# One plain round of the first feed-forward matrix instead of two, and six accumulators of the output projection held between its last two passes

## The chip, the cores and the metric

The kernel runs on one core of a Trainium2 chip. The metric is the device time of one execution in microseconds. A core has a matrix engine (PE, TensorE), three engines for element-wise work (DVE or VectorE, ACT or ScalarE, POOL or GpSimd) and a queue engine that issues most loads (SP). Matrix products are accumulated in PSUM, which has eight banks of 128 partitions x 512 float32; everything else lies in SBUF.

## What is computed

Two layers of an encoder trunk on x of 512 frames x 1024 features, all in float32. Each layer mixes three groups of heads (windowed attention, forgetting attention, mLSTM) and then applies a feed-forward part:

```python
def _layer(x, norm1, w_in, ..., w_out, norm2, w_ff1, w_ff2):
    z = _rms(x, norm1) @ w_in
    ...
    x = x + jnp.concatenate([ya, yb, yc], axis=-1) @ w_out
    u = _rms(x, norm2) @ w_ff1
    return x + jnp.square(jax.nn.relu(u)) @ w_ff2
```

ya has the features 0 to 511 of the concatenation, yb 512 to 767, yc 768 to 1023. In tiles of 128 that is k = 0 to 3, 4 and 5, 6 and 7. w_out is 1024 x 1024, w_ff1 1024 x 4096, w_ff2 4096 x 1024.

## The kernel before

**Products in three parts.** Every large operand is split into a rounded half `hi` and a rest `lo`, and a product is three matmuls, hi x hi, hi x lo and lo x hi (`mm3`, L262 to L265). Weights come by DMA as tiles of 128 x 1024 (a *job*). `prep_part` makes `whi` on ScalarE (L205) and `wlo` on VectorE (L206). `getjob` hands out the next job in the order of the list `jobs` and has the two after it prepared; three pairs of `whi` and `wlo` exist. `load_ahead` keeps the loads going as far as there are free buffers (three `raw`, and in the feed-forward four `fraw` and, later, `xt` and `ms`).

**Output projection.** The last part of the generator `big_work` (L573 to L592) runs over the passes of `WPASS`, k = 0 to 3, then 4 and 5, then 6 and 7, and in each over four column groups `hf` of 256 features. Each group takes two banks. At the end of each group in each pass, VectorE adds the two banks to the residual `xT` (L587). In the last pass `xprep` then makes the halves `xh` (ScalarE, L334) and `xl` (VectorE, L335) of the gained x, which the feed-forward reads. The marks `wo0`, `wo1` and `wo2` tell when a pass has been issued. After `wo0`, `c_tail(0)` transposes the first half of the mLSTM output (L1007) and splits it as k = 6 (L1008, L1009); after `wo1`, `c_tail(1)` does so with the second half, k = 7. Then the buffers of the mixing part are released, those of the feed-forward opened, and the third pass is issued.

**Feed-forward, first matrix.** The 4096 hidden features are cut into `NR` = 8 rounds of 512, two to a group `s`. A round runs in one of two ways. The plain way (`ff1_std`, L1214) multiplies everything: four units of one job and 48 matmuls of 256 columns. The other way (`ff1_st`, L1245) is Strassen's, in Winograd's form: seven units of one job and 24 matmuls of 256 columns, on sums of blocks of x and of the weights. The sums of x come from `xsums` (L350) in eight steps. Those of the weights come partly from a second load that adds in the buffer (L160, issued by GpSimd) and partly from VectorE (L216 and L220). Both ways leave the squared ReLU in `ct`, from which `csplit`, `n1_`, `n2_`, `gsplit` and `tail_` (L1180 to L1206) make sums and their halves for the second matrix. The first `NSTD` = 2 rounds are plain.

In the Strassen way the sixth unit's bank X is read by VectorE (L1270), and the seventh unit adds to the same bank.

**Feed-forward, second matrix.** `ff2(s)` (L1306) runs Strassen's way over group s, 14 units of 24 matmuls, seven for each half `dg` of the output. VectorE adds each result to `xT` (L1294). Group 0 first multiplies the residual by `nv`, minus the mean square of x (L1293); the last group multiplies by `r2`, its reciprocal (L1296). So the second norm is applied after the matrices.

**The order.** L1359 to L1377 set it: first the 4 x `NSTD` plain units, with `sqacc` after the first of them (the sum of the squares, L326 to L330), `xsums` from the second on, two steps a unit, and `emit_r2` (L1121) after the fourth, which makes `nv` and `r2`. Then `ff_pairs` (L117) takes turns between units of `ff2` and of the remaining rounds; `LEAD` rounds' units could go ahead, and `LEAD` is 0. The order on each engine is set when the program is built: by and large the order of the code, with work moved ahead where an engine would wait.

Of the kernel before, what the change touches and what calls it, by code (L numbers as in the profile page):

```python
# [16 lines left out]
ALU = mybir.AluOpType  # L17
# [28 lines left out]
NSTD = 2  # L46
# [4 lines left out]
def trunk(ctx, tc, x, cols, rows, gate_w, tabs, w_in, w_out, w1, w2, out):  # L51
# [49 lines left out]
    LEAD = 0  # L101
# [349 lines left out]
    for l in range(L):  # L451
# [79 lines left out]
        def big_work():  # L531
# [41 lines left out]
            for pi, (a, b) in enumerate(WPASS):  # L573
                for hf in range(4):
                    ps = [att() for _ in range(2)]
                    if b - a == 4 or hf % 2 == 0:
                        ws = getjob()
                    for k in range(a, b):
                        hi, lo = ws[k - a if b - a == 4 else hf % 2 * 2 + k - a]
                        for j in range(2):  # L580
                            cs_ = slice(j * P, (j + 1) * P)
                            mm3(ps[j], hi[:, cs_], lo[:, cs_], yhi(k), ylo(k), k == a, k == b - 1)
                        if k < b - 1:
                            yield 1.31
                    for j in range(2):
                        kx = hf * 2 + j
                        V.tensor_tensor(xT[:, kx], ps[j], xT[:, kx], ALU.add)  # L587
                        if pi == len(WPASS) - 1:
                            xprep(kx, g2(l, kx), xh, xl)
                    if hf == 3:  # L590
                        done.add(f"wo{pi}")
                    yield 1.31  # L592

# [500 lines left out]
        fill_to("wo1")  # L1094
        c_tail(1)
        close_phase()
# [19 lines left out]
        def bank():  # L1116
            return banks.popleft()
# [3 lines left out]
        def emit_r2():  # L1121
# [7 lines left out]
            A.activation(r2, lnv, AF.Exp, scale=-1.0)  # L1129
            V.tensor_tensor(lnv, nv, r2, ALU.mult)  # L1130
            V.scalar_tensor_tensor(r2, lnv, 2.0, r2, ALU.add, ALU.mult)
            rr_.update(nv=nv, r2=r2)
# [81 lines left out]
        def ff1_std(s, rr):  # L1214
            for i in range(2):
# [3 lines left out]
                for j in range(2):  # L1219
# [10 lines left out]
                    if j == 1:  # L1230
# [7 lines left out]
                        else:  # L1238
                            if rr:
                                units.extend(quads)  # L1240
# [4 lines left out]
        def ff1_st(s, rr):  # L1245
            X, Y = bank(), bank()
# [59 lines left out]
        def ff2(s):  # L1306
# [37 lines left out]
            for dg in range(2):  # L1344
# [10 lines left out]
                if s == 0 and dg:  # L1355
                    free_ff.append(ms_)
# [5 lines left out]
        for n_ in range(4 * NSTD):  # L1362
            next(gens[1])
            if n_ == 0:
                for kx in range(KT):
                    sqacc(kx, kx == 0)
            if n_ == 3:
                emit_r2()
            if n_ == 1:
# [6 lines left out]
        for which, u in ff_pairs():  # L1376
            next(gens[which])  # L1377
# [61 lines left out]
```

## Time and profile before

| | |
|---|---|
| runs shown | 1065.3, 1065.5, 1065.88 us, median 1065.5 |
| profiled execution, its own time | 1065.74 us |
| its span, first to last instruction | 1064.0 us |
| granted TensorE clock | 1.00 |
| loads in the feed-forward | 512 KB each, median 4.2 to 5.1 us to landing by SP, 6.3 to 7.8 by GpSimd |
| HBM, read and written | 147.86 MB and 2.13 MB |

The page of the profile gives times in microseconds, unless marked ns. L1294 is line 1294 of the kernel. "out<-in" names tiles without their numbers; all PSUM tiles are called `at`. A row of a timeline has the start, the duration, the engine, the line and the operation, and in brackets how long the engine had been idle before it and what ended that. Matmuls are pipelined and their ends modelled, so the distance from start to start tells more than the duration. VectorE's rows overlap by about 0.1 us in the same way.

### The profile page before, as it was taken

To read this page: it belongs to the slowest core of one execution; us is meant where nothing else is said; L and a number is where in the kernel's file an instruction comes from. 1 tells how busy PE (TensorE), PEld (TensorE's weight loads), DVE (VectorE), ACT (ScalarE), POOL (GpSimd) and SP (SyncE) were. 2 spreads that over 40 slices of the span, in tenths; PEclk is the share of its full clock that TensorE was granted. 3 is DMA by queue.
4 is the path that set the end of the run, shared out by engine and by line. 5 is a ranking of instruction groups with operands and counts; after the bars stand their busy time and mean duration, and the time that the engine had idled before them with its cause. 6 is when DMAs were issued, how large, how long until landed. Compare 5 with 4: busy or idle time off the path is not lost.

```text
span 1064.0 us, 21687 instructions
## 1 busy us (share of the span) xinstructions
PE 1053.7 (99%) x8768; PEld 1002.8 (94%) x8768; DVE 904.2 (85%) x1540; ACT 627.4 (59%) x1097; POOL 102.3 (10%) x154
## 2 busy tenths in 40 slices
PE   8999999999999999999999999999999999999998
PEld 8999977899999999999999998778999999999998
DVE  7696877899997988988977878688999888898797
ACT  6446655376666666567455467444766666666662
POOL 2030020100010000010002200101000101001000
PEclk9999999999999999999999999999999999999999
DMA  6523121165388687676135221213544886767752
GB/s 215 166 98 110 61 68 51 61 193 144 120 211 224 161 217 199 179 215 181 51 110 164 94 80 41 85 46 134 145 120 140 221 215 173 222 181 190 212 134 80
DMA packets 47365, 151.86 MB, mean 143 GB/s; under 512 B 5648, under 2 KB 8848, under 8 KB 47264
## 3 DMA queue, kind: packets, MB, share of 16 engines
q1 hardware_dynamic: 39056, 120.84, 34.0%
q0 software_dynamic: 8064, 29.36, 15.9%
q8 instruction: 69, 1.13, 0.4%
q14 instruction: 32, 0.26, 0.1%
q10 hardware_dynamic: 144, 0.26, 0.1%
HBM read 147.86 MB, written 2.13 MB: 141 GB/s over the span
## 4 chain that ended last, share of the span: by engine, by line
PE 85%; DVE 9%; ACT 3%; issue 1%; DMA 0%; SPq 0%; DVEq 0%
PE at L263 26%; PE at L265 26%; PE at L264 26%; DVE rt L726 2%; DVE wlo L206 2%; PE at L856 1%; PE at L898 1%; PE at L881 1%; ACT pe L769 1%; PE at L979 1%; DVE z L722 1%; DVE z L728 1%; PE at L756 1%; DMA raw<-in_w_in_dram 0%; DVE rb L407 0%
## 5 line engine op out<-in xcount | busy, mean ns | idle before, releaser
L205 ACT ACTIVATE whi<-raw 128x1024 fp32r<-128x1024 f32 (+1 forms) x130 | 136.2, 1048 | 114.6 <-PE at L264 87.8
L264 PE MATMUL at<-xhl,whi 128*128 128x256 f32 (+1 forms) x704 | 198.0, 281 | 0.0
L263 PE MATMUL at<-xhl,whi 128*128 128x256 f32 (+1 forms) x640 | 181.4, 283 | 0.0
L265 PE MATMUL at<-xhl,wlo 128*128 128x256 f32 (+1 forms) x640 | 180.4, 282 | 0.0
L263 PE MATMUL at<-yg,whi 128*128 128x256 f32 (+1 forms) x592 | 179.9, 307 | 0.5 <-DVE xT L1294 0.5
L206 DVE TENSOR_TENSOR wlo<-raw,whi 128x1024 fp32r<-128x1024 f32 (+1 forms) x130 | 157.4, 1211 | 27.0 <-ACT whi L205 26.6
L265 PE MATMUL at<-yg,wlo 128*128 128x256 f32 (+1 forms) x592 | 178.4, 301 | 0.0
L264 PE MATMUL at<-yg,whi 128*128 128x256 f32 (+1 forms) x560 | 169.4, 303 | 0.0
L263 PE MATMUL at<-whi,xhl 128*128 128x256 f32 (+1 forms) x576 | 163.0, 283 | 0.8 <-ACT xhl L334 0.7
L265 PE MATMUL at<-whi,xhl 128*128 128x256 f32 (+1 forms) x576 | 160.5, 279 | 0.6 <-DVE xhl L335 0.6
L264 PE MATMUL at<-wlo,xhl 128*128 128x256 f32 (+1 forms) x576 | 160.3, 278 | 0.5 <-DVE wlo L206 0.5
L205 ACT ACTIVATE whi<-fraw 128x1024 fp32r<-128x1024 f32 x100 | 106.1, 1061 | 83.9 <-PE at L264 79.6
L206 DVE TENSOR_TENSOR wlo<-fraw,whi 128x1024 fp32r<-128x1024 f32 x100 | 122.2, 1222 | 26.2 <-ACT whi L205 25.6
L264 PEld LDWEIGHTS at<-xhl,whi 128*128 128x128 f32 x704 | 132.2, 188 | 1.8 <-issue 0.5
L263 PEld LDWEIGHTS at<-xhl,whi 128*128 128x128 f32 x640 | 120.1, 188 | 1.7 <-ACT ct L1232 0.5
L265 PEld LDWEIGHTS at<-xhl,wlo 128*128 128x128 f32 x640 | 120.1, 188 | 1.2
L263 PEld LDWEIGHTS at<-yg,whi 128*128 128x128 f32 x592 | 111.2, 188 | 6.3 <-issue 1.7
L265 PEld LDWEIGHTS at<-yg,wlo 128*128 128x128 f32 x592 | 111.1, 188 | 5.3
L263 PEld LDWEIGHTS at<-whi,xhl 128*128 128x128 f32 x576 | 108.2, 188 | 1.8 <-ACT xhl L334 0.9
L264 PEld LDWEIGHTS at<-yg,whi 128*128 128x128 f32 x560 | 105.2, 188 | 4.2 <-DVE yg L1009 0.5
L265 PEld LDWEIGHTS at<-whi,xhl 128*128 128x128 f32 x576 | 108.2, 188 | 1.1 <-DVE xhl L335 1.0
L264 PEld LDWEIGHTS at<-wlo,xhl 128*128 128x128 f32 x576 | 108.4, 188 | 0.7 <-DVE wlo L206 0.7
(301 smaller groups left out, 2517.0 us busy)
## 6 DMA issues: line engine op xcount, KB each, us to landing
fraw<-in_w_dram SPq DMA_DIRECT2D x72, 512.0 KB, 4.9
raw<-in_w_dram SPq DMA_DIRECT2D x56, 512.0 KB, 4.3
raw<-in_w_in_dram SPq DMA_DIRECT2D x34, 512.0 KB, 3.5
fraw<-in_w_dram POOLq DMA_DIRECT2D x32, 512.0 KB, 6.3
raw<-in_w_out_dram SPq DMA_DIRECT2D x16, 512.0 KB, 3.2
xt<-in_w_dram SPq DMA_DIRECT2D x16, 512.0 KB, 5.1
raw<-in_w_dram POOLq DMA_DIRECT2D x14, 512.0 KB, 7.2
ms<-in_w_dram SPq DMA_DIRECT2D x12, 512.0 KB, 4.2
```

The lines of the kernel that those rows point to most:

```text
L205: A.activation(hi[:, cs_], raw[:, cs_], AF.Copy)
L206: V.tensor_tensor(lo[:, cs_], raw[:, cs_], hi[:, cs_], ALU.subtract)
L263: T.matmul(o, sh, mh, start=first, stop=False, skip_group_check=skip)
L264: T.matmul(o, sh, ml, start=False, stop=False, skip_group_check=skip)
L265: T.matmul(o, sl, mh, start=False, stop=last, skip_group_check=skip)
L722: V.tensor_tensor(z10, z10, bc(rq), ALU.mult)
L726: V.tensor_tensor(r10[:, oo:oo + n, a:a + 32], z10[:, oo:oo + n, b:b + 32], tb(S_, n, a, a + 32), ALU.mult)
L728: V.tensor_tensor(zaq[t], ro[:, :640], rt[:, :640], ALU.add)
L756: T.matmul(sc[r][:, g * 256:g * 256 + nk], qTA[g][r * 64:(r + 1) * 64, c * P:(c + 1) * P], kTA[r * 64:(r + 1) * 64, k0:k0 + nk], start=Tru ...
L769: A.activation(pe[:, u, :nk], sc[u % 2][:, (u // 2) * 256:(u // 2) * 256 + nk], AF.Exp, bias=nmx[:, u:u + 1], accum_out=ssum[:, u:u + 1])
L856: T.matmul(sp[:, :nk], qTB[rs, pr, n * P:(n + 1) * P], kTB[rs, pr, :nk], start=True, stop=False)
L881: T.transpose(pt[:, b * P:(b + 1) * P], scs[r][:, b * P:(b + 1) * P], ident)
```

## The change

`NSTD` becomes 1: the second round of each layer is computed in Strassen's way instead of the plain one. `LEAD` becomes 7: the seven units of that round run ahead of the first unit of `ff2`. `xsums` begins after the first plain unit and is through after the fourth; `sqacc` moves to behind the first Strassen unit and `emit_r2` to behind the fourth. The last two instructions of `emit_r2`, a correction of `r2`, become `finish_r2` and move to the end of `ff2(0)`. A bank that ScalarE seeds must be one that a matmul has written before.

In the output projection the first pass stays. Then the column groups 0, 1 and 2 take k = 4 and 5 into six banks that stay open, with `c_tail(1)` issued after the second of them, and `c_tail(0)` ahead of them as before. After the release of the buffers, groups 2, 0 and 1 take k = 6 and 7 into the same banks, and group 3 takes k = 4 to 7 at once. The host lays out the jobs of `w_out` to match, in the same number and size.

```diff
-NSTD = 2
+NSTD = 1
...
-    LEAD = 0
+    LEAD = 7
...
+            open_ = {}
+            for hf in range(3):
+                open_[hf] = [att() for _ in range(2)]
+                if hf != 1:
+                    ws = getjob()
+                for k in (4, 5):
+                    wo_part(open_[hf], ws[2 * (hf % 2) + k - 4], k, k == 4, False)
+                    if k == 5:
+                        done.add(f"wo1{hf}")
                     yield 1.31
+            for hf in (2, 0, 1, 3):
+                if hf == 3:
+                    open_[hf] = [att() for _ in range(2)]
+                if hf in (0, 3):
+                    ws = getjob()
+                for k in range(4 if hf == 3 else 6, 8):
+                    wo_part(open_[hf], ws[k - 4 if hf == 3 else (hf if hf < 2 else 1) * 2 + k - 6], k, hf == 3 and k == 4,
+                            k == 7)
+                    if k < 7:
+                        yield 1.31
+                wo_out(open_[hf], hf, True)
+                if hf == 3:
+                    done.add("wo2")
+                yield 1.31
...
-        fill_to("wo1")
+        fill_to("wo11")
         c_tail(1)
+        fill_to("wo12")
...
-        def bank():
-            return banks.popleft()
+        full = set()
+
+        def bank(seeded=False):
+            b = next(b for b in banks if not seeded or id(b) in full)
+            banks.remove(b)
+            full.add(id(b))
+            return b
...
+            rr_.update(nv=nv, lnv=lnv, r2=r2)
+
+        def finish_r2():
+            nv, lnv, r2 = (rr_[n] for n in ("nv", "lnv", "r2"))
             V.tensor_tensor(lnv, nv, r2, ALU.mult)
             V.scalar_tensor_tensor(r2, lnv, 2.0, r2, ALU.add, ALU.mult)
-            rr_.update(nv=nv, r2=r2)
...
-            X, Y = bank(), bank()
+            X, Y = bank(), bank(True)
...
                 if s == 0 and dg:
+                    finish_r2()
                     free_ff.append(ms_)
...
-        for n_ in range(4 * NSTD):
-            next(gens[1])
+        for n_, (which, u) in enumerate([(1, None)] * 4 * NSTD + list(ff_pairs())):
+            next(gens[which])
             if n_ == 0:
+                xt_ = wt("xt", "xt")
+                bg = xsums(l, *(v3(xt_[:, i * S:(i + 1) * S], 256) for i in range(2)))
+            if n_ < 4:
+                next(bg)
+                next(bg)
+            if n_ == 4:
                 for kx in range(KT):
                     sqacc(kx, kx == 0)
-            if n_ == 3:
+                free_ff.append(xt_)
+            if n_ == 7:
                 emit_r2()
```

`wo_part` holds the two `mm3` of a column group for one k, and `wo_out` the two adds of L587 and, where asked, `xprep`; both were written in place before.

More of the change, by code (lines that the diff above doesn't have):

```diff
@@ L572, in big_work, with wo_part @@
                 yield 1.31
[L573 to L591, printed above, removed]
-                    yield 1.31
+            def wo_part(ps, tiles, k, first, stop):
+                hi, lo = tiles
+                for j in range(2):
+                    cs_ = slice(j * P, (j + 1) * P)
+                    mm3(ps[j], hi[:, cs_], lo[:, cs_], yhi(k), ylo(k), first, stop)
@@ new lines, in wo_out @@
+            def wo_out(ps, hf, full):
+                for j in range(2):
+                    kx = hf * 2 + j
+                    V.tensor_tensor(xT[:, kx], ps[j], xT[:, kx], ALU.add)
+                    if full:
+                        xprep(kx, g2(l, kx), xh, xl)
+            for hf in range(4):
+                ps = [att() for _ in range(2)]
+                ws = getjob()
+                for k in range(4):
+                    wo_part(ps, ws[k], k, k == 0, k == 3)
+                    if k < 3:
+                        yield 1.31
+                wo_out(ps, hf, False)
+                if hf == 3:
+                    done.add("wo0")
+                yield 1.31
@@ L1238, in ff1_std @@
                         else:
-                            if rr:
+                            if rr == NSTD - 1:
                                 units.extend(quads)
@@ L1361, in trunk @@
         bg = None
-        for n_ in range(4 * NSTD):
-            next(gens[1])
+        for n_, (which, u) in enumerate([(1, None)] * 4 * NSTD + list(ff_pairs())):
+            next(gens[which])
             if n_ == 0:
+                xt_ = wt("xt", "xt")
[4 more added lines that the diff above has]
+            if n_ == 4:
                 for kx in range(KT):
                     sqacc(kx, kx == 0)
-            if n_ == 3:
+                free_ff.append(xt_)
+            if n_ == 7:
                 emit_r2()
-            if n_ == 1:
-                xt_ = wt("xt", "xt")
-                bg = xsums(l, *(v3(xt_[:, i * S:(i + 1) * S], 256) for i in range(2)))
-            if bg is not None:
-                next(bg, None)
-                next(bg, None)
-        free_ff.append(xt_)
-        for which, u in ff_pairs():
-            next(gens[which])
         close_phase()
@@ L1413, in _layout @@
         c = w_out[l].reshape(D, 4, 256).transpose(1, 0, 2)
-        t = [tiles(c, a, b - a) for a, b in WPASS]
-        wo.append(cc([t[0]] + [cc([t_[0::2], t_[1::2]], 2) for t_ in t[1:]], 0))
+        t, u, v = (tiles(c, a, b - a) for a, b in WPASS)
+        two = [cc(p, 1) for p in ((u[0], u[1]), (u[2], v[2]), (v[0], v[1]), (u[3], v[3]))]
+        wo.append(cc([t, np.stack(two)], 0))
     wo = np.stack(wo)
```

4 lines of the change are left out of this document (added).

## The prediction

> **What bounds the kernel now.** I read the page first: its busy shares, its forty slices, and the chain that ended last.
>
> ```profile
> PE 1053.7 (99%) x8768; PEld 1002.8 (94%) x8768; DVE 904.2 (85%) x1540; ACT 627.4 (59%) x1097; POOL 102.3 (10%) x154
> PE   8999999999999999999999999999999999999998
> DVE  7696877899997988988977878688999888898797
> PEclk9999999999999999999999999999999999999999
> PE 85%; DVE 9%; ACT 3%; issue 1%; DMA 0%; SPq 0%; DVEq 0%
> ```
>
> TensorE (PE) is busy 99% of the time at an undiminished clock, and 85% of the chain is its own work. But a busy PE is only a modelled end of pipelined matmuls, so I went to the view of stretches, with bounds at the stages of layer 0 (busy microseconds and instructions of each engine in each), and to PE's own list of waits, of which the last row below is one (total, times, longest).
>
> ```profile
> core 0: us, PE busy (x) PEld busy (x) DVE busy (x) ACT busy (x) POOL busy (x), PEclk, DMA share, GB/s
> 211.20:222.60 11.40, 11.40 (x53) 9.34 (x52) 10.21 (x16) 7.89 (x13) 0.00 (x0) 1.00 0.76 275
> 222.60:244.60 22.00, 22.00 (x195) 21.96 (x195) 21.83 (x38) 15.57 (x26) 1.89 (x2) 1.00 0.56 145
> 244.60:268.00 23.40, 23.40 (x203) 22.92 (x203) 23.29 (x32) 15.15 (x20) 1.72 (x2) 1.00 0.50 114
> 268.00:342.60 74.60, 74.60 (x661) 74.60 (x660) 65.09 (x70) 49.04 (x59) 6.04 (x7) 1.00 0.70 191
> ...
> PE at L264 <- DVE wlo L206: 0.5, 1, 0.5
> ```
>
> The first stretch is the last pass of the output projection, the next two are the two plain rounds, the last is group 0 of the second matrix. PE waits for nothing in any of them; over the whole run its worst wait for a weight half is 0.5 us, once. But VectorE (DVE) is full too through both plain rounds (21.83 of 22.00, 23.29 of 23.40), and has 9.5 us to spare only afterwards. So here PE is the bound and DVE is level with it: work taken from PE is time won only where DVE can follow.
>
> **The change, part by part.** The pitch of matmuls, not their modelled duration, prices PE. From the timeline of PE:
>
> ```profile
> 206.41 0.39 PE L263 MATMUL at<-yg,whi 128*128 128x512 f32 x1
> ...
> 210.49 0.39 PE L263 MATMUL at<-yg,whi 128*128 128x512 f32 x1
> ...
> 229.00 0.28 PE L263 MATMUL at<-xhl,whi 128*128 128x256 f32 x1
> ...
> 233.08 0.28 PE L263 MATMUL at<-xhl,whi 128*128 128x256 f32 x1
> ```
>
> Between the first two lie 18 matmuls of 512 columns (4.08 us, 0.227 each), between the last two 36 of 256 (0.1133 each). A plain round is 4 units of 48 such matmuls (5.44 us each), 192 in all; a Strassen round is 7 units of 24 (2.72 us each), 168. One round of each layer goes from the first kind to the second: 24 x 0.1133 = 2.72 us a layer, **5.44 us** for both. The output projection keeps its 192 matmuls, so PE gains nothing there. What DVE pays is priced by pitch as well:
>
> ```profile
> 228.13 0.48 DVE L364 SCALAR_TENSOR_TENSOR xt<-xT,pcol,xt 128x256 f32<-128x256 f32 x1
> 228.53 0.68 DVE L330 TENSOR_TENSOR accs<-accs,ms 128x512 f32<-128x512 f32 x1
> 229.13 0.48 DVE L364 SCALAR_TENSOR_TENSOR xt<-xT,pcol,xt 128x256 f32<-128x256 f32 x1
> ...
> 280.67 1.22 DVE L206 TENSOR_TENSOR wlo<-fraw,whi 128x1024 fp32r<-128x1024 f32 x1
> 281.81 1.22 DVE L220 TENSOR_TENSOR fraw<-raw,fraw 128x1024 f32<-128x1024 f32 x1
> ...
> 224.41 2.07 DVE L335 SCALAR_TENSOR_TENSOR xhl<-xT,pcol,xhl 128x512 fp32r<-128x512 f32 x3
> ```
>
> From start to start, 256 elements cost 0.40, 512 cost 0.60, 1024 cost 1.14; L335 costs about 0.66.
>
> Output projection: six fewer adds at L587 a layer, 3.6 us of DVE. They lay where PE did not wait, so by themselves they are worth nothing; what they buy is a shorter queue at the start of the feed-forward. Before, the last pass gave PE 48 matmuls (10.9 us) to eight adds and eight L335. Now the fourth group of columns runs all of k = 4 to 7 at the end, so the pass lasts 60 matmuls, 13.6 us. Its first three groups ask DVE for 3 x 2.5 us, and three weight halves 3.4: 10.9 of 13.6, 2.7 spare. The last group's 2.5 us always fall behind the start.
>
> The shortened start. Let T be the first matmul of the feed-forward. Plain units fill T to T+21.8; the seven leading Strassen units start every 2.72 us from there to T+40.8. In order of the code, DVE owes ahead of the weight half of the fourth leading unit (due at T+29.9): 2.5 left over; four weight halves, since they are made two units ahead, 4.6; the second unit's sum and half 2.3; all of the sums of x, 16 x 0.40 + 8 x 0.60 = 11.2; the plain round's splits and differences, 5 x 0.60 + 3 x 1.14 = 6.4; the norm's seven adds 4.2; that half 1.1. That is 32.3 us, **2.4 too many** a layer. Against it stand the 2.7 us spare before T, and these rows:
>
> ```profile
> 216.24 0.62 ACT L326 ACTIVATE accs<-xT 128x512 f32<-128x512 f32 x1
> ...
> 257.24 1.29 DVE L1293 SCALAR_TENSOR_TENSOR xT<-xT,ms 128x512 f32<-128x512 f32 x2
> ...
> 267.20 0.68 DVE L1293 SCALAR_TENSOR_TENSOR xT<-xT,ms 128x512 f32<-128x512 f32 x1
> 268.45 1.23 DVE L206 TENSOR_TENSOR wlo<-fraw,whi 128x1024 fp32r<-128x1024 f32 x1 [0.57 <-ACT whi L205]
> ```
>
> Work runs ahead of its place in the code wherever an engine is free: the first square (L326), issued in the code after the first plain unit, began 6.4 us before T (222.6). And all eight L1293, 4.8 us, were done by 268, though most are due much later; DVE then idled. So of what DVE had finished before, that much can slide. Bounds for this term: 0 and 2.4 us a layer. The rows of work done ahead are the nearer ones; I take 0.2.
>
> Leading round without second-matrix units between. In it L1270 reads the bank that the seventh unit adds to, right behind the sixth. Before, another unit (2.72 us) always lay between; no row shows it bare. The nearest is the end of the run, where the last half unit waits for a half-size eviction:
>
> ```profile
> 1057.72 0.28 PE L265 MATMUL at<-gx,wlo 128*128 128x256 f32 x1
> 1058.51 0.39 PE L263 MATMUL at<-yg,whi 128*128 128x256 f32 x1 [0.51 <-DVE xT L1294]
> ...
> 1058.04 0.42 DVE L1294 TENSOR_TENSOR xT<-xT,at 128x256 f32<-128x256 f32 x1
> ...
> L1270 DVE TENSOR_TENSOR ct<-at,ct 128x512 f32<-128x512 f32 x12 | 8.3, 692 | 6.1 <-PE at L265 6.1
> ```
>
> 0.79 from start to start instead of 0.11 is 0.68 lost around a 0.42 us add; L1270 takes 0.69, so 0.95 a layer, one end. The other end is 0, where other matmuls stand in the gap:
>
> ```profile
> 211.17 0.60 PE L1007 MATMUL at<-ident,yt 128*128 128x128 f32 x4
> ...
> 212.99 0.84 PE L263 MATMUL at<-yg,whi 128*128 128x512 f32 x3
> 213.67 0.39 PE L264 MATMUL at<-yg,whi 128*128 128x512 f32 x1
> ...
> 204.64 1.17 POOL L1000 TENSOR_TENSOR yt<-hs,co 128x64 f32<-128x64 f32 x4 [3.93 <-DVE hs L996]
> ```
>
> Three L263 in a row, where the code has L263, L264, L265 in turn, show that the order on PE was set to step over a half not ready yet; ready second-matrix units follow the seventh. Between 0 and 0.95 I take 0.3. The Trainium skill, "TensorE: Matmul & The Clock Gate", section "Step-by-step: what each phase is for", says that matmuls keep program order and only weight loads are pulled ahead. By that rule nothing fills the gap on the chip; unless the order of the build does, the sum below would be 1062.4 in place of 1061.1. No row here shows the gap itself.
>
> The moved transposes (L1007) come after two groups of 12 matmuls in place of four, 24 x 0.227 = 5.4 us earlier: 211.17 becomes 205.7, and yt was ready at 204.64 + 1.17 = 205.8. That is level; a dozen ready matmuls of the third group stand right behind and can step ahead as the L263 did: nothing, or some 0.2 us a layer if they do not. Moving the norm's correction behind the first ff2 group takes 1.2 us of DVE from the tight stretch, counted above by leaving it out. ScalarE was at 15.6 of 22.0 there: nothing. The leading round's seven loads are fewer than a pair of rounds moves in the same time later (191 GB/s): nothing, but if the summing loads came late, PE would wait for a landing of 6.3 us:
>
> ```profile
> fraw<-in_w_dram POOLq DMA_DIRECT2D x32, 512.0 KB, 6.3
> ```
>
> **The sum.** The profiled execution took 1065.74 us, 1.74 beyond its span of 1064.0, and the median is 1065.5. 1065.74 - 5.44 + 2 x (0.2 + 0.3) = 1061.3, or **1061.1** against the median.
>
> **The rivals.**
> 1. *Both stalls at their full price*: 2 x (2.4 + 0.95) = 6.7 given back for 5.44 won, 1066.8. For it: DVE full from 222.6 to 268. Against: the spare 2.7 us before T, and 4.8 us of L1293 that need not be early.
> 2. *A bank is late.* Six of the eight banks stay open. The fourth group needs two: the two that the transposes used are free by then, but if banks are taken in turn one or both are those of the first group, and PE waits for its adds at L587. Counted from the end of the second group in the last pass (which comes first there), these follow that group's own 2.5 us and cost 1.2, done at 3.7 of the 5.44 that two groups of 12 matmuls give. One weight half ahead makes 4.9, two make 6.0, 0.6 late; a second full set of adds 1.4 late. At 0.6 to 1.4 a layer: 1062.3 to 1063.9. The Trainium skill, "PSUM — Partial Sum Buffer", section "Summary: rules for kernel authors", asks to evacuate promptly; holding six banks goes against that, and this case would be its price here.
> 3. *DVE becomes the bound of the leading round, and the kernel gets slower.* If the eight L1293 (4.8) keep their early place, ahead of the weight halves, DVE is 2.4 + 4.8 = 7.2 us late a layer instead of 2.4: 1065.5 + 2 x (7.2 - 2.72) = 1074.5. It decides from 2.72 us of lateness a layer. For it: they did run early. Against: their factor now exists only after the fourth leading unit, and in the code they stand behind those halves.
> 4. *The saving does not come*: the matmuls go, but PE waits for landings (one of 6.3 us in each layer would eat 5.44 whole): about 1065.5 or more. Against: PE waits for no load anywhere in the feed-forward before.
>
> **How the numbers follow.** Forecast (within 1059.8 to 1063.0, from no stall to the whole bare gap): 0.68. Rival 1: 0.14; rival 2: 0.06; rival 3: 0.07; rival 4: 0.05. A measurement of this kernel tells about 0.2% (2.1 us) from no change, so faster is below 1063.4: the forecast, most of rival 2 and some of rival 1's milder half, 0.76. Within: the rest of rivals 1 and 2, and 4: 0.16. Slower: rival 3 and a long landing, 0.08. The range runs from the whole saving, 1059.8 with 0.3 us of scatter, to rival 1 at 1066.8.
>
> **What would show it.** PE has 8720 matmuls in place of 8768. If right, the two stretches before the first second-matrix unit are 2.7 us shorter in both layers, and PE's waits grow by under 1 us. A wait of PE for wlo (L206) in the leading round means rival 1 or 3; one for the add in L1270's place, the bare gap; one for the output projection's add ahead of its fourth group, rival 2; a weight conversion on ScalarE waiting for a DMA there, rival 4. The forecast is wrong if DVE, not PE, sets the pace from T+22 to T+41.

## The result and the profile after

The changed kernel is slower, and its times scatter. The kernel before gave 1065.72 us as the median of 18 executions (1065.3 to 1066.3). The changed one gave 1078.49, but the 18 times lie at three levels: two at 1065.25 and 1065.6, seven from 1073.98 to 1074.86, nine from 1082.13 to 1085.07. The ratio as compared is 1.0062 (95% interval 1.005 to 1.0074). It leaves out executions over 1.5% above the fastest, as disturbed ones, and so the whole upper level, though the granted clock was full there too (0.998 or more); the plain medians give 1078.49 / 1065.72 = 1.012. Forecast were 1061.1 us and a range of 1059.8 to 1066.8. The profiled execution took 1083.53 us, its span 1081.8. From its page, the busy times, the granted clock and the chain of waits:

```profile
PE 1068.5 (99%) x8720; PEld 1016.9 (94%) x8720; DVE 908.2 (84%) x1538; ACT 636.0 (59%) x1113; POOL 106.8 (10%) x158
PEclk9999999999999999999999999999999999999999
PE 77%; DVE 16%; ACT 4%; issue 2%; DMA 0%; SPq 0%; DVEq 0%
```

PE has 48 matmuls fewer, as foreseen, and yet 14.8 us more busy time, at the same granted clock. DVE takes 16% of the chain instead of 9%. Next the stretches of layer 0, with the columns of the table shown before, and PE's waits in them:

```profile
222.10:243.90 21.80, 21.80 (x193) 21.77 (x192) 21.66 (x37) 15.56 (x25) 0.86 (x1) 1.00 0.34 98
243.90:265.60 21.70, 19.92 (x168) 19.03 (x166) 20.33 (x27) 17.59 (x25) 1.72 (x2) 1.00 0.69 192
265.60:340.00 74.40, 74.35 (x643) 74.18 (x642) 68.52 (x76) 47.28 (x58) 6.23 (x8) 1.00 0.68 193
```

```profile
PE at L263 <- ACT at L1285: 1.2, 1, 1.2
PE at L265 <- DVE wlo L206: 0.6, 1, 0.6
```

In the leading round PE now idles for 1.78 of 21.70 us, where before it idled nowhere. Afterwards it idles hardly at all. So the waits explain some of the loss, but not 18 us of span. The rest is in the distance of matmuls, in two rows of PE's timeline with 17 others between them:

```profile
349.83 0.28 PE L263 MATMUL at<-xhl,whi 128*128 128x256 f32 x1
...
351.95 0.28 PE L263 MATMUL at<-yg,whi 128*128 128x256 f32 x1
```

18 matmuls in 2.12 us are 0.1178 each, where the prediction's rows had 0.1133. A wait shows as idle time, this does not: PE counts as busy and its clock as full. I took the distances of starts of all matmuls of each feed-forward part, from the start of its first matmul to the start of its last, and parted them at 0.135 us (longer: a wait, with the restart behind it):

| us | layer 0 before | after | layer 1 before | after |
|---|---|---|---|---|
| whole part | 311.16 | 320.02 | 311.77 | 321.87 |
| waits, beyond 0.1133 | 1.02 | 3.51 | 1.60 | 3.81 |
| pitch, beyond 0.1133 | 0.04 | 9.12 | 0.07 | 10.68 |

The 24 matmuls give 2.72 in each. Over both layers: 5.44 won, 4.70 lost in waits, 19.69 lost in the slower pitch. That makes 18.95, and the span grew by 17.8; the 1.15 between them lies outside the feed-forward, where the traces of single executions differ by as much (in those at the full clock its first matmul starts between 222.1 and 223.1). Without the last term the execution comes to 1065.74 - 5.44 + 4.70 = 1065.0, near the lowest level (1065.25). The levels, 9 us apart, fit none, one or two layers at the slower pitch: two in this trace, one in a second trace below (1075.08); no execution of the lowest level was profiled.

**The waits.** For the first, ScalarE's timeline, then PE's:

```profile
246.36 1.05 ACT L205 ACTIVATE whi<-fraw 128x1024 fp32r<-128x1024 f32 x1
247.31 1.05 ACT L1271 ACTIVATE ct<-ct 128x1024 f32<-128x1024 f32 x1
248.26 1.05 ACT L205 ACTIVATE whi<-raw 128x1024 fp32r<-128x1024 f32 x1
249.31 1.06 ACT L1220 ACTIVATE gx<-ct 128x1024 fp32r<-128x1024 f32 x1
250.27 0.58 ACT L1285 ACTIVATE at<-at 128x512 f32<-128x512 f32 x1
```

```profile
249.45 0.28 PE L265 MATMUL at<-xbx,wlo 128*128 128x256 f32 x1
250.91 0.39 PE L263 MATMUL at<-xbx,whi 128*128 128x256 f32 x1 [1.18 <-ACT at L1285]
```

The first leading unit's bank X is copied to Y (L1285), and the third unit adds to X, so it has to wait until the copy has read it. Before, a unit of the second matrix stood between two units of such a round. Now the copy has one unit, 2.72 us, and four operations of 1.05 us run one after another ahead of it on ScalarE: 1.34 us lost from start to start. For the second wait, DVE's timeline, then PE's:

```profile
259.56 1.21 DVE L206 TENSOR_TENSOR wlo<-raw,whi 128x1024 fp32r<-128x1024 f32 x1
260.70 0.69 DVE L1330 SCALAR_TENSOR_TENSOR xT<-xT,ms 128x512 f32<-128x512 f32 x1
261.30 0.69 DVE L1226 TENSOR_TENSOR yg<-ct,yg 128x512 fp32r<-128x512 f32 x1
261.90 0.68 DVE L1301 TENSOR_TENSOR ct<-at,ct 128x512 f32<-128x512 f32 x1
262.50 1.21 DVE L206 TENSOR_TENSOR wlo<-fraw,whi 128x1024 fp32r<-128x1024 f32 x1
```

```profile
262.89 0.28 PE L264 MATMUL at<-gx,whi 128*128 128x256 f32 x1
263.77 0.38 PE L265 MATMUL at<-gx,wlo 128*128 128x256 f32 x1 [0.60 <-DVE wlo L206]
```

The first second-matrix unit (gx) starts ahead of the seventh leading unit, and DVE, without a gap, makes its weight half 0.76 us late. One of the eight L1330 (L1293 before) stands ahead of it. A third wait, 0.21, comes at 301.73 in layer 0. In layer 1 the second wait is 0.56, and there is no third.

### The profile page after: what moved, and what is told of

It is laid out like the page before. It is cut to its first block, busy times and chain, and to the rows that moved or that the text cites. A ratio compares the mean times of both kernels' runs of the same rounds, so it can differ in the third digit from the quotient of the medians.

```text
span 1081.8 us, 21621 instructions
## 1 busy us (share of the span) xinstructions
PE 1068.5 (99%) x8720; PEld 1016.9 (94%) x8720; DVE 908.2 (84%) x1538; ACT 636.0 (59%) x1113; POOL 106.8 (10%) x158
## 4 chain that ended last, share of the span: by engine, by line
PE 77%; DVE 16%; ACT 4%; issue 2%; DMA 0%; SPq 0%; DVEq 0%
PE at L263 23%; PE at L265 23%; PE at L264 23%; DVE wlo L206 3%; DVE rt L754 2%; PE at L884 1%; PE at L926 1%; DVE accs L330 1%; PE at L909 1%; DVE xhl L335 1%; ACT pe L797 1%; ACT whi L205 1%; PE at L1007 1%; DVE z L750 1%; DVE z L756 1%
## 5 line engine op out<-in xcount | busy, mean ns | idle before, releaser
L205 ACT ACTIVATE whi<-raw 128x1024 fp32r<-128x1024 f32 (+1 forms) x136 | 142.3, 1046 | 114.5 <-PE at L264 85.1
L206 DVE TENSOR_TENSOR wlo<-raw,whi 128x1024 fp32r<-128x1024 f32 (+1 forms) x136 | 164.2, 1207 | 32.1 <-ACT whi L205 31.9
L263 PE MATMUL at<-yg,whi 128*128 128x256 f32 (+1 forms) x592 | 183.1, 311 | 0.5 <-DVE xT L1331 0.5
L264 PE MATMUL at<-xhl,whi 128*128 128x256 f32 (+1 forms) x624 | 177.9, 285 | 0.0
L264 PE MATMUL at<-yg,whi 128*128 128x256 f32 (+1 forms) x560 | 171.2, 306 | 0.0
L263 PE MATMUL at<-xhl,whi 128*128 128x256 f32 (+1 forms) x560 | 161.0, 288 | 0.0
L265 PE MATMUL at<-xhl,wlo 128*128 128x256 f32 (+1 forms) x560 | 160.0, 286 | 0.0
L206 DVE TENSOR_TENSOR wlo<-fraw,whi 128x1024 fp32r<-128x1024 f32 x102 | 124.4, 1219 | 26.7 <-ACT whi L205 26.6
L263 PE MATMUL at<-xbx,whi 128*128 128x256 f32 x448 | 126.0, 281 | 2.4 <-ACT at L1285 2.3
L264 PE MATMUL at<-xbx,whi 128*128 128x256 f32 x448 | 125.5, 280 | 0.0
L265 PE MATMUL at<-xbx,wlo 128*128 128x256 f32 x448 | 125.5, 280 | 0.0
L264 PEld LDWEIGHTS at<-xhl,whi 128*128 128x128 f32 x624 | 117.9, 189 | 1.8 <-issue 0.5
```

The costliest lines, as they stand in the source:

```text
L205: A.activation(hi[:, cs_], raw[:, cs_], AF.Copy)
L206: V.tensor_tensor(lo[:, cs_], raw[:, cs_], hi[:, cs_], ALU.subtract)
L263: T.matmul(o, sh, mh, start=first, stop=False, skip_group_check=skip)
L264: T.matmul(o, sh, ml, start=False, stop=False, skip_group_check=skip)
L265: T.matmul(o, sl, mh, start=False, stop=last, skip_group_check=skip)
```

## The experiments

The theory (A): the change brings back waits where DVE and ScalarE no longer follow, and beyond their length a wait can move PE from one pitch to another, which then stays. Rivals: the output projection is to blame (B); the slower pitch belongs to places in the program (C) or to the changed rounds alone (D).

### Which part of the change

**The projection alone**: the new projection, the old feed-forward (two of the lines that differ from the changed kernel).

```diff
-NSTD = 1
+NSTD = 2
-    LEAD = 7
+    LEAD = 0
```

> Only the output projection is changed (two plain rounds stay). Theory A (what was lost is lost in the leading round: PE stalls there, and after a stall its matmuls go on at 117.7 ns from start to start in place of 113.3 until something puts them back): no new stall, 1065.5 within 0.5, all executions alike. Theory B (the held accumulators and the new order of groups cost it): 4 to 17 us slower than before, executions spread.

Median 1065.4 (1065.16 to 1065.88), ratio 1.0 (0.9991 to 1.0009), no slower pitch in the feed-forward of its trace. B falls: holding six accumulators neither costs nor brings anything here.

**The rounds alone**: the old projection, the new feed-forward (lines that differ from the changed kernel).

```diff
...
-            open_ = {}
-            for hf in range(3):
...
+            for pi, (a, b) in enumerate(WPASS):
+                for hf in range(4):
...
```

> Only the rounds are changed (one plain, seven leading units), the projection in three passes as before. Theory A: the same two stalls a layer as with the whole change (1.3 us for the seeding copy, 0.7 us or some more for a weight half, since VectorE starts with about 1 us more in its queue), and the same spread of executions at about 1065, 1074 and 1083. Theory B: 1060 to 1061, executions alike.

Six executions from 1066.14 to 1068.02, four from 1076.65 to 1076.94; ratio 1.0049 (1.0019 to 1.008). The loss and the levels come with the rounds. The waits lie elsewhere (1.69 us around the norm's matmul at 253.06, 0.81 at 257.59, none for the copy), and one layer of the profiled execution is at the slower pitch.

### The waits

**The copy first**: on ScalarE the copy goes ahead of the square that needs nothing of it.

```diff
...
+            cp = A.activation(Y, X, AF.Copy)
+            if (s, rr) == (0, 1):
+                tc.add_manual_dep(rr_["sq"].ins, cp.ins.name, mybir.DependencyInfo(
+                    mybir.DependencyClass.NoSync, mybir.DependencyReason.DATA), reason="copy first")
```

> The whole change, with ScalarE's seeding copy ordered ahead of the square of the plain round. Theory A: PE's wait of 1.3 us for that copy goes in both layers, so an execution in which the pitch stays at 113.3 ns takes about 1062.5; the waits for a weight half (0.7 us a layer) and the short one a round later stay, and with them the spread by 8 to 10 us a layer. If the copy was the only trigger of the slow pitch: 1062.5 in every execution. If the pitch has nothing to do with waits: the same spread as before, 2 to 3 us lower.

Five executions from 1064.07 to 1064.51, five from 1074.45 to 1075.35; ratio 1.0038 (1.0005 to 1.0071). The copy's wait is gone, the third level too. The second wait grew, in PE's timeline:

```profile
262.34 0.28 PE L264 MATMUL at<-gx,whi 128*128 128x256 f32 x1
263.73 0.39 PE L265 MATMUL at<-gx,wlo 128*128 128x256 f32 x1 [1.12 <-DVE wlo L206]
```

DVE is just as late, and PE arrives earlier. Counted as in the table above, the waits of the profiled execution come to 7.28 us in both layers, against 7.32 without the edit: what the copy's wait gave up, the second wait (now 1.28 a layer) and three short ones behind the norm's matmul took. The lower levels still lie 1.1 us apart; no trace says why. This version's lower level is under the kernel before (1064.28 against 1065.43), in half of its executions.

**Five leading units instead of seven**, with the copy first and the norm's scale one unit later:

```diff
-    LEAD = 7
+    LEAD = 5
-            if n_ == 7:
+            if n_ == 8:
```

> As the one before, and five units lead instead of seven: units of the second matrix stand between the last two of the leading round, and the mean square is made after the fifth unit instead of the fourth, so that the residual's multiplications cannot come ahead of so many weight halves. Theory A: if no wait of PE is left between the plain round and the end of the feed-forward, 1060.3 to 1061 and all executions alike; with a wait of some tenths left, 1061 at the low end and 8 to 10 us a layer more in others. Rival (VectorE as such is too slow for the shortened start): the wait for a weight half stays, at 0.7 us a layer or more.

Three executions from 1064.24 to 1065.2, two near 1068.6, five from 1074.16 to 1075.12, ratio 1.0047 (1.0019 to 1.0074). A wait of 1.1 us now comes at 255.53, ahead of the norm. **The norm's scale three units later**, behind the last of seven leading units and with the copy first, so that the L1330 come later:

```diff
-            if n_ == 7:
+            if n_ == 10:
```

> The changed kernel with the copy first, and with the norm's scale made after the tenth unit of the list instead of the seventh, so that the eight products of residual and mean square (L1330 of the changed kernel) come later on VectorE. With the copy first alone, 1.28 us of waiting for the first weight remainder of the second matrix was left in each layer. If those eight, run early, hold that remainder back (the mechanism of the forecast's rival 3), the wait goes and the lowest times fall from 1064.1 by up to 2.6 us, to 1061.5 to 1062.5. If VectorE is simply full in this stretch whatever comes first, the wait moves to another place and the lowest times stay at 1063.8 to 1064.6. In both, executions some 10 us longer are still seen if any wait is left in front of the long row of products.

1065.55, 1075.40 and 1083.97 us, and 1158.51 at a granted clock of 0.85. The waits moved to 255.05 (1.10, for a weight half), 262.47 (1.22) and 280.26 (0.31), and did not shrink: all waits of layer 0 make 3.9 us, 3.4 with the copy first alone. The first L1330 (L1333 here) now runs at 270.12, behind the first two of them (the third has one right ahead of it), so the early L1330 alone do not hold PE up. The wait at 262.47 is the gap that the prediction called bare: PE waits for the add that reads bank X (L1310 here), with one product of the second matrix in between. That DVE has no room in this stretch whatever comes first is likely and not shown; it idled 0.26 us ahead of the weight half at 261.28.

**The eight multiplications on GpSimd** (with the copy first and five leading units):

```diff
...
-                V.scalar_tensor_tensor(t_, t_, -1.0, bc_("nv"), ALU.mult, ALU.mult)
+                G.tensor_tensor(t_, t_, bc_("nv"), ALU.mult)
```

> As the one before, and the residual's multiplications run on GpSimd (plain products with the positive mean square; the correction of its reciprocal takes one instruction more). Theory A with VectorE as the cause of the waits: 4.8 us of VectorE a layer go, no wait of PE is left, 1060.3 to 1061, all alike. If GpSimd is so slow that the additions behind those products come late, PE waits for banks: above 1066.

1079.6 to 1094.81, ratio 1.022 (1.0177 to 1.0263). From the timelines of GpSimd and of DVE:

```profile
262.80 15.73 POOL L1334 TENSOR_TENSOR xT<-xT,ms 128x512 f32<-128x512 f32 x8 [2.11 <-ACT ct L1230]
```

```profile
270.01 0.68 DVE L1311 TENSOR_TENSOR ct<-at,ct 128x512 f32<-128x512 f32 x1
...
272.23 1.78 DVE L1168 TENSOR_TENSOR ms<-ms,r 128x512 f32<-128x512 f32 x1
```

GpSimd takes 2 us for each, and while it works DVE's 512-element operations on two SBUF operands take 1.78 instead of 0.68; those with an operand in PSUM (`at`) keep 0.68. PE's waits in layer 0 grow to 11.0 us, from 3.0 with five leading units alone, and in each layer the granted clock is halved once behind such a wait (0.50 from 805.2 to 808 in layer 1). The Trainium skill, "SBUF — State Buffer", section "SBUF: two separate sides", states that the two engines share a port pair, which one holds for a whole instruction, also against VectorE operations with two SBUF inputs; the rows agree on which operations are held up.

### The pitch

**The changed kernel again**, nothing altered.

> The changed kernel once more, for a second trace of the same program. Theory A: the waits of PE in the leading rounds are the same within 0.1 us, and the stretches at 117.7 ns begin and end only at waits, but not necessarily at the same ones; the time is near 1065, 1074 or 1083, and 4.4 ns for every matmul at the slow pitch make up the difference. Theory C (pitch by place in the program): the same stretches are slow.

1075.08 us. From the stretches of the first trace and then of this one:

```profile
280.00:300.00 20.00, 20.00 (x179) 20.00 (x178) 20.00 (x24) 11.53 (x14) 0.86 (x1) 1.00 0.55 168
340.00:360.00 20.00, 20.00 (x172) 20.00 (x172) 19.95 (x21) 13.54 (x17) 2.42 (x3) 1.00 0.61 142
1000.00:1020.00 20.00, 20.00 (x172) 20.00 (x171) 16.11 (x17) 11.20 (x13) 2.60 (x3) 1.00 0.69 183
```

```profile
280.00:300.00 20.00, 20.00 (x172) 20.00 (x171) 20.00 (x24) 10.72 (x13) 0.85 (x1) 1.00 0.56 164
340.00:360.00 20.00, 20.00 (x172) 20.00 (x172) 19.57 (x21) 13.65 (x17) 2.59 (x3) 1.00 0.59 136
1000.00:1020.00 20.00, 20.00 (x179) 20.00 (x179) 14.58 (x16) 10.82 (x14) 2.59 (x3) 1.00 0.93 232
```

179 matmuls in 20 us is the one pitch, 172 the other (a stretch also counts those that reach into it). Same program, and nearly the same waits: the copy's is 1.33 or 1.34 in all four layers, the second 0.55 or 0.56 here (0.76 and 0.56 in the first trace), and the third comes in layer 1 here. In the first execution the pitch of layer 0 changed at the third wait (301.73) to slow; layer 1 began fast and was slow for good from behind its second wait (799.5). In this one layer 0 became slow for good behind the second wait (263.06, with a break of 0.09 at 265.55, which the first execution had too and passed at the fast pitch), while layer 1 was fast from behind that place (801) to the end. C falls. What differs is visible in the loads of weights between 350 and 420, grouped by line (count, busy us, mean ns): the first trace, this one, the kernel before.

```profile
L264 PEld LDWEIGHTS at<-xbx,whi 128*128 128x128 f32 x56 | 10.8, 192 | 0.0
L263 PEld LDWEIGHTS at<-xbx,whi 128*128 128x128 f32 x56 | 10.5, 188 | 0.0
```

```profile
L263 PEld LDWEIGHTS at<-xbx,whi 128*128 128x128 f32 x56 | 10.8, 192 | 0.0
L264 PEld LDWEIGHTS at<-xbx,whi 128*128 128x128 f32 x56 | 10.5, 188 | 0.0
```

```profile
L264 PEld LDWEIGHTS at<-xbx,whi 128*128 128x128 f32 x64 | 12.0, 188 | 0.0
```

At the slower pitch one of the three loads of each product takes 192 ns, the same one through these rows: the second in the first trace, the first in the other.

**One plain matmul ahead of each second-matrix group**, in the changed kernel:

```diff
+                if dg == 0:
+                    T.matmul(X[dg][:, :P], ones_m, ones_m, start=True, stop=True)
```

> The whole change, and at the start of each of the four groups of the second matrix one more matmul of two plain float32 tiles of 128 x 128, whose result is overwritten. Theory A, with the guess that such a matmul puts the pitch back to 113.3 ns: slow stretches end at the next group, 77 us at most, so 1064 to 1068 and no execution over 1070, though PE has more to do. If the pitch is not put back by it: 1065 to 1085 in the same three levels plus 1. Theory C (the pitch goes with banks and addresses, so with the place in the program): the slow stretches stay where they were, 1075 to 1085.

1075.18 to 1078.05, ratio 1.0102 (1.0086 to 1.0119): one level. My guess that it brings the fast pitch back was wrong. In the trace each of the six that stand within a steady row *reverses* the pitch (in layer 0 slow from 344, fast from 424, slow from 500). **The same edit in the kernel before**, once and then with a second such matmul behind each:

> The kernel before, untouched but for one plain fp32 128x128 matmul put in front of each of the four groups of the second matrix in each layer (8 in all, on a bank that the next product clears; the output is unchanged). No wait is added. Theory A (TensorE has two pitches, 113.3 and 117.7 ns, and an interruption of the row of products, such as a plain matmul, can move it from one to the other; the kernel before merely has no interruption there): each inserted matmul reverses the pitch, so about half of each layer runs slow: about 8 x 0.35 = 2.8 us for the matmuls themselves and some 4.5 to 6 us a layer, 1076 to 1081 us, always the same, and pitch rows at 0.118 in two of the four groups. Rival D (the slower pitch comes from the changed rounds alone): 1068.3 us, 113.3 ns throughout.

> As the run with one plain matmul ahead of each group, but with two, one right behind the other. If a plain matmul reverses the pitch each time, the second puts it back: 113.3 ns throughout, 1065.5 + 8 x 0.6 = about 1070.3 us (1069 to 1072), all executions alike. If it only draws the pitch anew, the executions differ from one another by several us, between 1070 and 1090 us. Rival D (only the changed rounds have the slower pitch) also gives about 1070 here, so this run counts only beside the one with one plain matmul.

One matmul: 1078.57, 1079.34 and 1080.75 (a fourth took 2134.60 and is left out), ratio 1.0129 (1.0111 to 1.0148). Two: 1068.41 to 1069.31 in seven, ratio 1.0031 (1.0019 to 1.0042). The stretches within the four groups of layer 0, with one and then (a single row) with two:

```profile
270.00:290.00 20.00, 20.00 (x172) 20.00 (x171) 18.97 (x20) 11.76 (x13) 0.00 (x0) 1.00 0.36 118
360.00:380.00 20.00, 20.00 (x179) 20.00 (x178) 17.11 (x19) 11.30 (x14) 2.60 (x3) 1.00 0.70 185
430.00:450.00 20.00, 20.00 (x172) 20.00 (x171) 17.25 (x19) 11.53 (x14) 1.73 (x2) 1.00 0.64 170
510.00:530.00 20.00, 20.00 (x179) 20.00 (x178) 19.72 (x24) 8.88 (x11) 0.00 (x0) 1.00 0.16 54
```

```profile
430.00:450.00 20.00, 20.00 (x179) 20.00 (x178) 17.92 (x19) 12.31 (x16) 1.73 (x2) 1.00 0.63 162
```

Slow, fast, slow, fast; with two, fast throughout. So the kernel before has the second pitch too: eight short matmuls cost it 14 us, sixteen cost 3. D falls. Even untouched it shows that pitch, in a short row with other operands: the input products of layer 1, of which the stretch from 534 to 545 holds 95, against 99 in as long a stretch of the feed-forward, with the loads from 535 to 544 as here:

```profile
L264 PEld LDWEIGHTS at<-wlo,xhl 128*128 128x128 f32 x26 | 5.0, 192 | 0.0
```

There the pitch changes without a break, where the operands change.

**A wait in the kernel before.** A detour of 128-column matmuls ahead of the second group, without a wait and then with one (the loop stands in the second of the two runs alone):

```diff
+                if (s, dg) == (1, 0):
+                    T.matmul(X[dg][:, :P], xh[:, 0, :P], xh[:, 0, :P], start=True, stop=True)
+                    A.activation(ctl, X[dg][:, :P], AF.Copy)
+                    for _ in range(4):
+                        G.tensor_copy(ctl, ctl)
+                    T.matmul(X[dg][:, :P], xh[:, 0, :P], ctl, start=True, stop=True)
```

> The kernel before, with a short detour of TensorE ahead of the second group of the second matrix in each layer: one 128x128 fp32r matmul into the bank that the next product clears, ScalarE copies its result out, and a second 128x128 matmul multiplies the copy. The output is unchanged. Thirteen matmuls of another unit stand between the two, 1.5 us, so the second waits little or not at all. It is the control for the next run. If the two extra matmuls by themselves do nothing to the pitch: 1065.5 + 2 x 0.2 = 1065.9 us, all executions alike. If a matmul of another width by itself moves the pitch as the plain one does: the third and later groups slow in both layers, about 7 us a layer, 1080 us.

> As the run before in this list, with four copies on GpSimd behind ScalarE's, so that TensorE, with nineteen matmuls (2.2 us) in between, has to wait for the second extra matmul, once a layer, in the kernel before. Theory A (a wait can move the pitch, whatever kernel it is in): beyond the waits' own time (from 0 to 2 us a layer) executions lie at two or three levels about 7 us apart, or all at a level 7 or 14 us up, with rows at 117.7 ns behind the wait. Rival D (the slower pitch needs the changed rounds): all executions alike, at 1065.9 us and the waits' own time.

Without: nine executions from 1066.37 to 1067.02 (the profiled one took 1311.69 at a granted clock of 0.75, where the two pitches can't be told apart). With: 1081.39 to 1087.15. From PE's timeline of the second, and its stretches:

```profile
349.76 0.47 PE L1317 MATMUL at<-ctl,xhl 128*128 128x128 f32 x1 [3.48 <-POOL ctl L1316]
```

```profile
350.00:352.00 2.00, 2.00 (x10) 2.00 (x11) 0.78 (x1) 0.00 (x0) 0.00 (x0) 0.50 0.04 8
400.00:420.00 20.00, 20.00 (x172) 20.00 (x172) 13.68 (x15) 11.51 (x15) 1.29 (x2) 1.00 0.74 205
1000.00:1020.00 20.00, 20.00 (x179) 20.00 (x178) 19.00 (x20) 13.71 (x17) 1.75 (x2) 1.00 0.71 190
```

In both layers the first extra matmul turned the pitch slow (0.118 ahead of the wait). Where the second follows without a wait, the times fit that it turns back. Behind the wait one layer stayed slow, the other was fast: the wait broke the pattern, in the kernel before. The levels foretold do not stand out in four executions, since the waits themselves were 3.6 and 5.6 us, longer than the 2 us expected, and the granted clock was 0.50 behind both.

**A matmul of the norm's width behind the waits**, meant to bring the fast pitch back: in the changed kernel, with the copy first, and there again one product earlier (the lines are those of the first two runs).

```diff
+                if (s, dg) == (0, 1):
+                    T.matmul(Y, ones_m, ones_m.unsqueeze(1).broadcast_to((P, 4, P)), start=True, stop=True)
```

> The changed kernel with one more plain fp32 matmul of 512 columns a layer, of the norm's form, in the middle of the first group of the second matrix, behind the last of the waits (on a bank that the next product clears; the output is unchanged). In every trace so far the row behind the norm's own matmul runs at 113.3 ns, four times out of a row at 117.8. Theory A (the excess is the slower pitch, entered at a wait, and such a matmul ends it): the three levels fall together; lowest level 1065.3 + 2 x 0.7 = 1066.7 us, and at most 40 us a layer at the slower pitch ahead of it (1.6 us a layer), so every execution lies between 1066.5 and 1070. If that matmul only reverses or draws the pitch, as the short one does, executions near 1076 and 1084 stay.

> The changed kernel with the copy first, and with the same matmul of 512 columns in the same place. With the copy first alone the executions lay at 1064.2 and 1074.8. Theory A: all between 1065.3 and 1069 us, none near 1075. Otherwise: two levels again, each some 1.4 us higher.

> As the run before in this list, but the 512-column matmul stands one product earlier in the list, directly behind the wait for the first weight remainder of the second matrix (at 265 to 272 us instead of 305), so that nothing of the long row is left ahead of it. Theory A: one level at 1064.2 + 1.4 = 1065.6 us (1065.3 to 1066.2), unless a further wait comes behind it; with one, an execution in a few near 1075.

The first gave 1068.26 and four from 1075.74 to 1077.7, the second 1069.62 to 1084.22 (half of ten near 1083.8), the third 1077.34 and three near 1085.5. The idea fell, and how it fell supports the reversal. The stretches ahead of and behind it in the first, layer 0 and then layer 1:

```profile
285.00:305.00 20.00, 20.00 (x172) 20.00 (x171) 20.00 (x25) 12.24 (x16) 1.73 (x2) 1.00 0.66 189
310.00:330.00 20.00, 20.00 (x179) 20.00 (x178) 16.33 (x17) 10.53 (x13) 2.58 (x3) 1.00 0.85 231
812.00:832.00 20.00, 19.95 (x177) 19.78 (x176) 20.00 (x25) 11.71 (x16) 1.74 (x2) 1.00 0.66 195
836.00:856.00 20.00, 20.00 (x173) 20.00 (x172) 17.45 (x18) 10.62 (x12) 2.16 (x3) 1.00 0.83 242
```

It turned slow into fast and fast into slow. With the copy first, where half of the executions had been at the lower level, half are now near 1083.8, and the trace of one is slow in both layers behind that matmul. (The rows behind the norm itself were at 113.3 ns wherever one could be read, three times, not four as I wrote, out of the slower pitch.)

**Waits or addresses alone, outside the layers.**

```diff
+    for g in range(48):
+        if g % 4 == 3:
+            T.matmul(bk, ones_m, xr[:, 1], start=True, stop=True)
+        unit()
+        A.activation(dst[:, :n], bk[:, :n], AF.Copy)
```

> Nothing of the layers is computed: one bank, 48 times 96 matmuls of the kernel's kind (128 x 128 weights, 256 columns, weight half, weight half, rest), each time after a wait for a ScalarE copy of 32, 128, 256 or 512 columns out of that bank; every fourth time a plain float32 matmul of 512 columns follows the wait. Theory A: same instructions and addresses each time, but the pitch of a stretch is 113.3 or 117.7 ns and changes only at a wait; behind the plain matmul it is always 113.3. Theory C: one pitch throughout.

611.63 us, and every row but the first at 119.8 to 119.9 ns, whatever the wait: neither theory's picture. There all three loads of a product take 192 ns. So waits do not suffice; the next run varied where the operands lie:

```diff
+    PADS = (0, 8, 16, 32)
...
+    wl = [wb[:, 2048 * (k + 1) + p:2048 * (k + 1) + p + D] for k, p in enumerate(PADS)]
+    xl = [xb[:, 1024 * (k + 1) + p:1024 * (k + 1) + p + S] for k, p in enumerate(PADS)]
...
+                T.matmul(bk[:, :P], ones_m, ones_m, start=True, stop=True)
+                unit(wl[i], xl[j])
```

> The layers are left out: 48 rows of 96 fp32r matmuls (128x128 weights, 256 columns, three to a product as in the layers), one after another without a wait, one plain fp32 128x128 matmul ahead of each. The remainder of the weights lies 0, 8, 16 or 32 elements off the pitch of the weights' high part, that of the columns likewise: 16 pairs, three rows each. If the pitch hangs on where the operands lie, the rows of some pairs have another pitch than those of others (113.3, 117.7 or the 120 ns of the run with waits alone). If it hangs on the plain matmul in front alone, the three rows of one pair differ. If neither, all 48 are at 120 ns.

Worked out from the starts, the three rows of a pair agree within 0.25 ns in 13 of the 16 pairs (without the very first row, at the start), and the pairs differ (offset of the weights first): 120.0 ns with both offsets 0 or 0 and 8, 117.8 with 0 and 32, 118.4 with 8 and 0. In two the rows alternate, as a reversal would have it (117.8, 119.8, 117.8 with 32 and 16; 117.8, 116.6, 117.8 with 16 and 32). None has 113.3. A plain matmul stands ahead of every row, so in 13 pairs it reverses nothing. Two stretches, the rows with 0 and 8 and those with 8 and 8; the second holds nearly as many matmuls in 33 us as the first in 34:

```profile
44.00:78.00 34.00, 34.00 (x286) 34.00 (x285) 0.00 (x0) 0.00 (x0) 0.00 (x0) 1.00 0.00 1
...
184.00:217.00 33.00, 33.00 (x283) 33.00 (x282) 0.00 (x0) 0.00 (x0) 0.00 (x0) 1.00 0.01 1
```

So which pitches there are hangs on the addresses of the operands. Where there are two, as in the layers, a break in the row can move PE from one to the other; not each break does.

## Why the prediction was wrong

- **The saving** (5.44 us): the count was right, 8720, and the lowest level, 1065.25, is about what it leaves after the waits.
- **The output projection** at nothing: right, as the run with it alone shows. Rival 2 did not come about: PE's list of waits has none for that add (L582 in the changed kernel). The Trainium skill, "PSUM — Partial Sum Buffer", section "Summary: rules for kernel authors", asks to evacuate promptly; here six banks held over two passes cost nothing measurable. Rival 4 did not either: PE waits for no load there.
- **The bare gap** (0.3 taken of 0 to 0.95): 0 in the changed kernel. The order of the build put the first product of the second matrix there, 262.78 to 265.59. But that asked for its weight half a unit earlier, and this became the second wait. In the run with the norm later the gap did show, at 1.22 us in layer 0, over the upper bound.
- **DVE's lateness** (0.2 taken of 0 to 2.4): about 0.6 to 1.0 a layer in the two traces, inside the bounds and three to five times the size. The rows of work that DVE had done early were the wrong ones to lean on; in the run with the norm later the lateness moves and stays.
- **ScalarE, "at 15.6 of 22.0 there: nothing"**: this step failed outright. It went by a busy share, where the operations that stand ahead of the awaited one should have been counted: four of 1.05 us stood ahead of the copy, and PE lost 1.34 us a layer. Setting the copy first removed this wait.
- **The pitch**: the step that sank the forecast. "The pitch of matmuls prices PE" set 0.1133 for every matmul, behind a wait as before it, so that a wait cost its length. The waits lost 4.70 us, which with the saving leaves about 1065, hardly a change; the 9 and 18 us of the upper levels are matmuls at 0.1177. No term of the sum and no rival had that, and without it the time would have been in the stated range, near its upper end.
- **Rival 3** had the right sign, and at 1074.5 the middle level, by luck, since its mechanism is another: it wanted DVE 7.2 us late a layer by early L1330. DVE was late by about one, and with the L1330 later the levels stayed.

What is shown: the waits arise with the rounds; the copy's order made one; every lasting change of pitch in the feed-forward of the changed kernel's two traces stands at a break in the row of products; a single plain matmul within a steady row reverses the pitch in either kernel, and eight of them cost the one before 14 us. What stays open: why one load in three then takes 4 ns more while a product of three matmuls takes 13 ns more, by which rule of addresses, why one break changes the pitch and another does not, and whether another placement of the operands would have no second pitch. A version without waits was not reached: each edit moved them.

## What to carry to other kernels

Where PE runs hundreds of microseconds without a break, the break may cost far more than its length: compare the starts of matmuls behind it with those ahead of it, and look at the times of many executions, not at their median. Before work is taken from PE, list for each operation that PE will then wait for what stands ahead of it in its engine's queue; a busy share says nothing about that. Here an engine that was nearly full beside PE gave the saving back elsewhere, whichever wait was mended first.

## What the hardware showed

- Two pitches of the same fp32r matmul (128 x 128 weights loaded each time, 256 columns) at a granted clock of 1.00: 113.3 and 117.7 ns. The slower one goes with one load in three at 192 instead of 188 ns. In the feed-forward's rows a pitch held from one break to the next (2345 matmuls at 117.8 behind 799.5 in the first trace), and a single plain matmul of 128 or 512 columns in a steady row reversed it. With other addresses there are rows at 116.6 to 120.0 ns, and there a plain matmul mostly changed nothing. The Trainium skill, "TensorE: Matmul & The Clock Gate", section "Back-to-back issue gap", gives N / 2.4 + 2.5 ns for the gap of isolated matmuls, by which an estimate for 256 columns is 109, and says that in a stream the loads share in the spacing; no pitch measured here is as short, and the section has no second one.
- Behind a wait of 3.48 us the granted clock was halved (0.50 in the rows at 350) for twelve matmuls, 213 ns each; behind waits of 1.3 us it was not. In the run with GpSimd a gap of 2.63 us between starts (801.91 to 804.54) was followed by 0.50 from 805.2 on, and one of 2.64 (from 268.20) by none. The Trainium skill, "TensorE: Matmul & The Clock Gate", section "Part 1: The HAM clock gate", puts the slower state behind at least one idle window of about 3.4 us; the wait of 3.48 agrees, the gap of 2.63 does not, and here the measurement decides.
